# Attention value products of two heads in one call, in the two halves of the array's columns

## The chip, the core and the metric

The kernel runs on one core of one Trainium2 chip. The metric is the device time of one execution in microseconds (us). The engines of the core have their own instruction streams: TensorE (PE) multiplies matrices, VectorE (DVE) and ScalarE (ACT) work on vectors, GpSimd (POOL) is not used for the computation, and SyncE (SP) issues the transfers from the main memory. TensorE writes its results to PSUM, which here is used as eight banks of 128 x 512 fp32 numbers.

## The reference

Two layers, each of a gated feed-forward block, a mixer of three branches, and a second feed-forward block, on 256 positions of width 1024, all in fp32. The mixer's middle branch is latent attention; this is the part that matters here:

```python
def attend(args):                          # for each block of 128 queries
    qn, qp, blk = args
    sc = (einsum('bqhd,bkhd->bhqk', qn, k_nope) + einsum('bqhr,bkr->bhqk', qp, k_pe)) * scale
    sc = where(key_idx[None, :] <= q_idx[:, None], sc, finfo(float32).min)
    p = softmax(sc, axis=-1)
    return einsum('bhqk,bkhd->bqhd', p, v)   # 8 heads, 64 value columns each
o = o.swapaxes(0, 1).reshape(b, s, 8 * 64)
return o @ w_o
```

The other two branches of the mixer are a gated linear recurrence and a depthwise convolution over 31 positions with a layer norm. The three are gated, added and projected.

## The kernel before

All weights are cut into blocks of 128 x 128 and packed in the order of their use, eight blocks to a chunk of 512 KB. A chunk is fetched into one of 7 buffers (`raw`), ACT rounds it to fp32r (`wh`), and DVE computes the rest (`wl`), each into one of 5 buffers. A product of activations and weights is three fp32r matmuls (`gemm`: high by high, high by low, low by high), over 256 columns each. Some small products are done in plain fp32: the sums over rows by a matrix of ones, the attention scores, and the attention values.

The program is recorded first (line 397 is the line of the recorder that issues each instruction, so nearly all rows name it) and then ordered by a planner. TensorE keeps the order in which the program was written. For the other engines `set_due` (line 426) works out backwards, from a table of costs (`cost`, line 366), when each operation is due, and `schedule` (line 468) plays the program through with these costs and takes, on each engine, the ready operation that is due first. A different cost of one kind of matmul moves all due times.

The attention of one layer is spread over eleven steps (`attend`, line 991), which are placed between the tiles of the gates' and output projections by `ATT_AT` (line 38). A step s issues, in this order: the scores of head s; the values of head s - 3; the transposes of head s - 2; the last part of the softmax of head s. The names in the profile: `kt`, `qt` are keys and queries, `s` the softmax's tile (128 queries x 384: the first 128 columns are the first block of queries, which sees only the first 128 keys), `st` its sums, `ptt` its transpose as ACT copies it out of PSUM (two buffers), `vt` the values (keys x heads), `o` the result of two heads in fp32r for the output projection. `xg` and `ya` are activations that the projections around the steps read.

In `values` (line 978) the weights of the array are 64 columns of `vt`, and the output is 64 partitions of a PSUM tile: the even head of a pair goes to partitions 0 to 63, the odd one to 64 to 127. Two matmuls make one head: the first 128 keys by all 256 queries, and the second 128 keys by the second 128 queries. The scores' weights are 128 columns wide, and so are the transposes' and the projections'.

In the mixer's opening, well ahead of the attention, come the convolution branch's input tiles (`c2`, then `c1`, both `c` in the order's rows, `cin` their product), two sums of squares for the norms of queries and keys (`rv`, `ry`, `rt` belong to their reciprocal square roots), and the copies of the rotated keys into `kt`.

Of the kernel before, what the change touches and what calls it, by code (L numbers as in the profile page):

```python
# [12 lines left out]
F32R = mybir.dt.float32r  # L13
# [5 lines left out]
P = 128  # L19
S = 256  # L20
# [5 lines left out]
H = 8  # L26
NOPE, ROPE, VD = 64, 32, 64
# [300 lines left out]
class Op:  # L328


    def __init__(self, at, engine, call, cost, table):
        self.at, self.engine, self.call, self.cost, self.table = at, engine, call, cost, table
        self.before, self.after, self.buffers = set(), set(), []
        self.due, self.start, self.end = 0.0, None, None
# [7 lines left out]
class Program:  # L342
# [23 lines left out]
    def cost(self, engine, method, args, kw, out, ins):  # L366

        n = out.size if isinstance(out, View) else ins[0].size
        sbuf = all(not v.buf.pool.psum for v in ins)
        column = lambda v: isinstance(v, View) and v.size == 1  # L370
        if engine == "sync":
            return max(0.45, n * 4 * P / 360e3)
        if engine == "tensor":
            return n / 2400 + (0.0133 if n < 512 else 0.018) if args[1].buf.dt == F32R else n * 4 / 2400 + 0.005
        if engine == "scalar":
            t = n / 1200 + (0.093 if sbuf else 0.06) + (0.09 if "accum_out" in kw else 0)
            return t + (0.1 if column(kw.get("scale")) else 0) + (0.06 if column(kw.get("bias")) else 0)
        if engine == "gpsimd":
            return 0.15 + n * 0.0018
        if method == "tensor_scalar" and sbuf and n > 16:  # L380
            return n / 1920 + 0.08
        t = (6 if method == "reciprocal" else 1) * n / 960 + 0.069
        return t + (0.06 if sbuf and any(map(column, ins)) else 0)
# [173 lines left out]
def mixer_kernel(ctx: ExitStack, tc: tile.TileContext, ws, xt, par, pos, out):  # L557
    program = Program(tc.nc)
    V, A, G, T, sync = (program.engine(n) for n in ("vector", "scalar", "gpsimd", "tensor", "sync"))
# [11 lines left out]
    def ps():  # L571
        return psp.tile([P, 512], F32, name="ps")
# [3 lines left out]
    def bt(name="bt"):  # L576

        rest = halves.pop(name, None)
        if rest is None:
            both = big.tile([P, 2, S], F32, tag="pair", name=name, parts=2)  # L580
            rest, halves[name] = both[:, 0, :], both[:, 1, :]
        return rest
# [6 lines left out]
    pts = [cst.tile([P, b - a], F32, name=f"par{a}") for a, b in zip(cuts, cuts[1:])]  # L589
# [53 lines left out]
    def split(src, scale=None, name="sp", pool=None):  # L643

        pool = pool or big
        both = pool.tile([P, 2, S], F32R, tag="pair", name=name, parts=2)
        h, lo = both[:, 0, :], both[:, 1, :]
        if scale is None:
            A.activation(h, src, AF.Copy)
            V.tensor_tensor(lo, src, h.bitcast(F32), op=SUB)  # L650
        else:
            A.activation(h, src, AF.Copy, scale=scale)
            V.scalar_tensor_tensor(lo, src, scale, h.bitcast(F32), op0=MUL, op1=SUB)
        return both
# [120 lines left out]
    def mixer(l, norm, nxt):  # L775
# [28 lines left out]
        t = W_IN_ORDER[2]  # L804
# [64 lines left out]
        for i in range(4):  # L869
            A.activation(xin[:, i, :], mm(f"xa{i}"), AF.Identity, bias=bias(f"xa{i}"))  # L870
            t = bt(name="xa")
# [6 lines left out]
        for i in range(4):  # L878
            t = bt(name="gel")
# [12 lines left out]
        for k in range(2):  # L892
            h, lo = W.block("v", l, k, 0, width=4)
            xh, xl = (normed[f"kv{k}"][:, i, :] for i in range(2))
            for t in range(2):
                c = slice(t * P, (t + 1) * P)
# [3 lines left out]
        vt = mixp.tile([P, 2, 512], F32, name="vt", parts=2)  # L900
# [5 lines left out]
        for i in range(4):  # L906
# [6 lines left out]
            c = 4 * l + i  # L913
# [13 lines left out]
        for h in range(H):  # L927
# [3 lines left out]
            t = bt(name="qt")  # L931
# [11 lines left out]
            yas.append(split(gel[i], name="ya"))  # L943


        sm, pts, ot, os_ = {}, {}, {}, {}

        def scores(h):
            k = kt[h % 2][:, h // 2, :]
            acc = ps()  # L950
            T.matmul(acc[:, 0:P], qt[h][:, 0:P], k[:, 0:P], start=True, stop=True)
            T.matmul(acc[:, P:3 * P], qt[h][:, P:S], k, start=True, stop=True)
            s = attp.tile([P, 3 * P], F32, tag="s", name="s")
            st = attp.tile([P, 4], F32, tag="st", name="st")
            mask = whole("mask")
            for i, c in ((0, slice(0, P)), (1, slice(P, 3 * P))):
                V.tensor_tensor_reduce(out=s[:, c], in0=acc[:, c], in1=mask[:, c], scale=1.0, scalar=3e38,
                                       op0=ADD, op1=ALU.min, accum_out=st[:, i:i + 1])
            for i, c in ((0, slice(0, P)), (1, slice(P, 3 * P))):
                A.activation(s[:, c], s[:, c], AF.Exp, bias=st[:, i:i + 1], scale=-1.0, accum_out=st[:, 2 + i:3 + i])  # L960
            sm[h] = (s, st)

        def normalise(h):
            s, st = sm[h]
            V.reciprocal(st[:, 2:4], st[:, 2:4])
            A.activation(s[:, 0:P], s[:, 0:P], AF.Copy, scale=st[:, 2:3])
            A.activation(s[:, P:3 * P], s[:, P:3 * P], AF.Copy, scale=st[:, 3:4])

        def transposes(h):
            s, _ = sm.pop(h)  # L970
            acc = ps()
            for i in range(3):
                T.transpose(acc[:, i * P:(i + 1) * P], s[:, i * P:(i + 1) * P], whole("ident"))
            t = ptp.tile([P, 3 * P], F32, tag="pt", name="ptt")
            A.activation(t, acc[:, 0:3 * P], AF.Copy)
            pts[h] = t

        def values(h):
            p, e = divmod(h, 2)
            if e == 0:  # L980
                ot[p] = ps()[:, :S]
            o = ot[p][64 * e:64 * e + 64]
            t = pts.pop(h)
            T.matmul(o, vt[:, 0, h * VD:(h + 1) * VD], t[:, 0:S], start=True, stop=False)
            T.matmul(o[:, P:S], vt[:, 1, h * VD:(h + 1) * VD], t[:, S:3 * P], start=False, stop=True)
            if e == 1:
                os_[p] = split(ot.pop(p), name="o")

        step = [0]

        def attend():
            s = step[0]
            step[0] += 1
            if s < H:
                scores(s)
            if 0 <= s - 3 < H:
                values(s - 3)
            if 0 <= s - 2 < H:
                transposes(s - 2)
            if s < H:  # L1000
                normalise(s)

        def slot(n):
            if n in ATT_AT:
                attend()
# [65 lines left out]
        while step[0] < H + 3:  # L1071
            attend()
# [18 lines left out]
        pair = [ps() for _ in range(2)]  # L1091
# [85 lines left out]
    for l in range(DEPTH):  # L1177
        mix, second = Norm(f"gm_{l}"), Norm(f"g2_{l}")
        ffn("ffn1_", l, norm, mix, constants if l == 0 else None)
        mixer(l, mix, second)  # L1180
        norm = Norm(f"g1_{l + 1}" if l + 1 < DEPTH else "gf")
        ffn("ffn2_", l, second, norm)
# [33 lines left out]
```

## Time and profile before

| | before |
|---|---|
| device time, median of 3 runs | 1218.55 us (1218.47 to 1218.88) |
| profiled execution | 1218.95 us |
| its span, first to last instruction | 1217.0 us |
| PE busy | 1199.6 us (99%) |
| DVE busy | 952.7 us (78%) |
| ACT busy | 774.5 us (64%) |

The span lies inside the device time; what is around it is start and end of the program. Busy time counts an engine's instructions and not its waits. In the page's timeline by slices PE is at 9 tenths or more in all but the first and last of 40 slices. The ends of matmuls in the trace are modelled, so the length of a matmul's record is longer than the time that the next one has to wait; what a matmul costs is read from the distance of two starts.

### The profile page before, as it was taken

The numbers are of one execution on the slowest core, as the hardware profiler recorded it, in microseconds if no ns is written. First come the engines' busy times: TensorE is split into PE (matmuls) and PEld (weight loads), VectorE is DVE, ScalarE is ACT, GpSimd is POOL, SyncE is SP. The second block draws the span as 40 slices with busy tenths as digits, with TensorE's granted clock in tenths as the row PEclk, the third lists the DMA queues.
The fourth block names the chain that finished last, engine by engine and source line by source line (L and its number), as shares of the span: only waits on it lengthen the run. The fifth ranks groups of instructions, "written<-read, shape, count | busy, mean of one in ns | idle before, by whom it ended". The sixth has DMA issues, their size and how long they took to land.

```text
span 1217.0 us, 21025 instructions
## 1 busy us (share of the span) xinstructions
PE 1199.6 (99%) x8018; PEld 1095.7 (90%) x8018; DVE 952.7 (78%) x1750; ACT 774.5 (64%) x1326; POOL 0.2 (0%) x4
## 2 busy tenths in 40 slices
PE   7999999999999999999999999999999999999997
PEld 6888889999999898888898888899999999988886
DVE  7976667999987986776686676689999699866653
ACT  7655545889657765555465565468896577655552
POOL 0000000000000000000000000000000000000000
PEclk9999999999999999999999999999999999999999
DMA  8655555554445655555555555546544556555540
GB/s 306 222 191 190 181 191 166 191 173 146 157 166 166 197 178 190 189 191 191 178 186 191 191 186 186 186 156 203 174 153 134 179 162 199 184 190 189 190 140 35
DMA packets 61157, 218.17 MB, mean 179 GB/s; under 512 B 6912, under 2 KB 7936, under 8 KB 61056
## 3 DMA queue, kind: packets, MB, share of 16 engines
q1 hardware_dynamic: 61056, 216.82, 54.3%
q8 instruction: 63, 1.03, 0.3%
q14 instruction: 38, 0.31, 0.1%
HBM read 215.75 MB, written 1.05 MB: 178 GB/s over the span
## 4 chain that ended last, share of the span: by engine, by line
PE 98%; DMA 1%; ACT 0%; DVE 0%; SPq 0%; issue 0%; DVEq 0%
PE ps L397 98%; DMA xs<-xt 1%; SPq L397 0%; ACT wh L397 0%; DVE y L397 0%; ACT xg L397 0%; ACT sq L397 0%; DVE wl L397 0%; DVE rt L397 0%; DVEq L1211 0%; ACT ry L397 0%; DVE r L397 0%; DVE rv L397 0%; DVE xs L397 0%
## 5 line engine op out<-in xcount | busy, mean ns | idle before, releaser
L397 PE MATMUL ps<-xg,wh 128*128 128x256 f32 (+1 forms) x3136 | 757.7, 326 | 8.3 <-ACT wh L397 8.3
L397 DVE TENSOR_TENSOR wl<-raw,wh 128x1024 fp32r<-128x1024 f32 (+1 forms) x412 | 498.2, 1212 | 198.1 <-ACT wh L397 196.2
L397 ACT ACTIVATE wh<-raw 128x1024 fp32r<-128x1024 f32 (+1 forms) x412 | 430.9, 1047 | 276.5 <-PE ps L397 153.5
L397 PE MATMUL ps<-xg,wl 128*128 128x256 f32 x2144 | 579.2, 281 | 0.5 <-DVE wl L397 0.5
L397 PEld LDWEIGHTS ps<-xg,wh 128*128 128x128 f32 x3136 | 517.7, 191 | 49.0 <-ACT wh L397 8.5
L397 PEld LDWEIGHTS ps<-xg,wl 128*128 128x128 f32 x2144 | 407.9, 190 | 13.6 <-DVE wl L397 0.9
L397 PE MATMUL ps<-hid,wh 128*128 128x512 f32 (+1 forms) x726 | 247.0, 391 | 0.0
L397 PE MATMUL ps<-hid,wl 128*128 128x256 f32 x704 | 192.7, 281 | 0.0
L397 PEld LDWEIGHTS ps<-hid,wh 128*128 128x128 f32 x726 | 133.2, 188 | 29.1
L397 PEld LDWEIGHTS ps<-hid,wl 128*128 128x128 f32 x704 | 133.1, 189 | 2.7
L397 DVE SCALAR_TENSOR_TENSOR conv<-cin,taps,conv 128x255 f32<-128x255 f32 (+28 forms) x240 | 100.0, 464 | 1.6 <-ACT conv L397 1.3
L397 ACT ACTIVATE s<-s 128x256 f32<-128x256 f32 x88 | 35.8, 414 | 62.6 <-DVE s L397 62.6
L397 ACT ACT_TABLE_LOAD x37 | 47.5, 1283 | 1.3 <-PEq L1205 0.7
L397 ACT ACTIVATE s<-s,st 128x128 f32<-128x128 f32 x64 | 28.0, 451 | 26.7 <-DVE st L397 26.7
L397 PE MATMUL ps<-mg,wh 128*128 128x512 f32 x128 | 44.4, 397 | 0.0
L397 DVE SCALAR_TENSOR_TENSOR xs<-ps,xs 128x256 f32<-128x256 f32 x63 | 26.6, 422 | 22.2 <-PE ps L397 21.4
L397 DVE TENSOR_TENSOR hid<-hid 128x256 fp32r<-128x256 f32 x88 | 36.2, 417 | 0.0
L397 ACT ACTIVATE hid<-hid 128x256 fp32r<-128x256 f32 x88 | 35.3, 409 | 0.0
L397 ACT ACTIVATE sq<-xs 128x256 f32<-128x256 f32 x49 | 19.8, 405 | 23.1 <-DVE xs L397 19.6
L397 PE MATMUL ps<-mg,wl 128*128 128x256 f32 x128 | 33.4, 279 | 0.0
L397 DVE TENSOR_TENSOR u<-ps,u 128x256 f32<-128x256 f32 x72 | 30.1, 418 | 3.7 <-ACT u L397 3.7
L397 DVE TENSOR_TENSOR hid<-u,s 128x256 f32<-128x256 f32 x72 | 30.6, 425 | 2.3
(164 smaller groups left out, 1010.9 us busy)
## 6 DMA issues: line engine op xcount, KB each, us to landing
raw<-ws SPq DMA_DIRECT2D x406, 512.0 KB, 3.4
out<-y SPq DMA_DIRECT2D x4, 256.0 KB, 2.3
par<-par SPq DMA_DIRECT2D x1, 571.0 KB, 8.4
raw<-ws SPq DMA_DIRECT2D x4, 128.0 KB, 3.6
xs<-xt SPq DMA_DIRECT2D x1, 512.0 KB, 7.0
raw<-ws SPq DMA_DIRECT2D x2, 256.0 KB, 7.1
xs<-xt SPq DMA_DIRECT2D x2, 128.0 KB, 2.9
xs<-xt SPq DMA_DIRECT2D x1, 256.0 KB, 4.1
```

The source lines that it names most:

```text
L397: getattr(getattr(self.nc, engine), method)(*map(put, args), **{k: put(v) for k, v in kw.items()})
```

## The change

`values` takes a pair of heads p instead of one head, and is called in the steps 4, 6, 8 and 10 instead of in the steps 3 to 10. In a call the two matmuls over the first keys are issued for the even and then the odd head, and then the two over the second keys. So the even head's values are issued one step later than before, the odd head's in the same step. The planner's cost of a matmul whose weights have 64 columns is multiplied by 0.6. Nothing else is changed in the program's text.

```diff
@@ cost
         if engine == "tensor":
-            return n / 2400 + (0.0133 if n < 512 else 0.018) if args[1].buf.dt == F32R else n * 4 / 2400 + 0.005
+            t = n / 2400 + (0.0133 if n < 512 else 0.018) if args[1].buf.dt == F32R else n * 4 / 2400 + 0.005
+            return t * 0.6 if args[1].shape[-1] == 64 else t
@@ mixer
-        def values(h):
-            p, e = divmod(h, 2)
-            if e == 0:
-                ot[p] = ps()[:, :S]
-            o = ot[p][64 * e:64 * e + 64]
-            t = pts.pop(h)
-            T.matmul(o, vt[:, 0, h * VD:(h + 1) * VD], t[:, 0:S], start=True, stop=False)
-            T.matmul(o[:, P:S], vt[:, 1, h * VD:(h + 1) * VD], t[:, S:3 * P], start=False, stop=True)
-            if e == 1:
-                os_[p] = split(ot.pop(p), name="o")
+        def values(p):
+
+            o = ps()[:, :S]
+            pair = [(64 * e, 2 * p + e, pts.pop(2 * p + e)) for e in range(2)]
+            for c, h, t in pair:
+                T.matmul(o[c:c + 64], vt[:, 0, h * VD:(h + 1) * VD], t[:, 0:S], start=True, stop=False)
+            for c, h, t in pair:
+                T.matmul(o[c:c + 64, P:S], vt[:, 1, h * VD:(h + 1) * VD], t[:, S:3 * P], start=False, stop=True)
+            os_[p] = split(o, name="o")
@@ attend
-            if 0 <= s - 3 < H:
-                values(s - 3)
+            if s >= 4 and s % 2 == 0:
+                values((s - 4) // 2)
```

On PE, step 3 of the first layer's attention, between the tiles of a gate projection, stands so in the order before (the numbers behind names are buffer numbers):

```order
L397 MATMUL ps<-xg,wl 128x256
L397 MATMUL ps<-kt_2643,qt 128x128
L397 MATMUL ps<-kt_2643,qt 128x256
L397 MATMUL ps<-ptt,vt 64x256
L397 MATMUL ps<-ptt,vt 64x128
L397 MATMUL ps<-par_187,s 128x128 x3
L397 MATMUL ps<-xg,wh 128x256 x2
```

and so in the changed kernel, where the values are gone from this step:

```order
L398 MATMUL ps<-xg,wl 128x256
L398 MATMUL ps<-kt_2625,qt 128x128
L398 MATMUL ps<-kt_2625,qt 128x256
L398 MATMUL ps<-par_187,s 128x128 x3
L398 MATMUL ps<-xg,wh 128x256 x2
```

One step later on PE, step 4 of the first layer, the order before has one head's values, like step 3. In the changed kernel the values of two heads stand there:

```order
L398 MATMUL ps<-ya,wl 128x256
L398 MATMUL ps<-kt_2610,qt 128x128
L398 MATMUL ps<-kt_2610,qt 128x256
L398 MATMUL ps<-ptt,vt 64x256 x2
L398 MATMUL ps<-ptt,vt 64x128 x2
L398 MATMUL ps<-par_187,s 128x128 x3
L398 MATMUL ps<-ya,wh 128x256 x2
```

The planner's new cost also moves instructions on DVE and ACT (303 and 110 lines of difference in their orders; PE's has 50). The largest move on ACT is in the opening of the first layer's mixer, where `c` are the evictions of the convolution branch's tiles. Before:

```order
L397 ACTIVATE conv<-cin,par_187,taps_264 128x256
L397 ACTIVATE wh<-raw 128x1024
L397 ACTIVATE c_2581<-ps,hb_261 128x256
L397 ACTIVATE kt_2589<-ps 64x1024
L397 ACT_TABLE_LOAD
L397 ACTIVATE ry<-ps,par_187 128x256 x2
L397 ACTIVATE wh<-raw 128x1024
L397 ACTIVATE kt_2643<-ps 64x1024
L397 ACTIVATE c_2655<-ps,par_187 128x256
```

and in the changed kernel:

```order
L398 ACTIVATE conv<-cin,par_187,taps_264 128x256
L398 ACTIVATE wh<-raw 128x1024
L398 ACT_TABLE_LOAD
L398 ACTIVATE ry<-ps,par_187 128x256 x2
L398 ACTIVATE kt_2610<-ps 64x1024
L398 ACTIVATE kt_2625<-ps 64x1024
L398 ACTIVATE wh<-raw 128x1024
L398 ACT_TABLE_LOAD
L398 ACTIVATE c_2655<-ps,hb_261 128x256
```

The eviction that stood ahead of the copies and the two `ry` now stands behind them and behind a second table load.

## Rows read from the trace of the kernel before

**Rows 1.** The page's head and its first part: busy us, share, instructions.

```profile
span 1217.0 us, 21025 instructions
PE 1199.6 (99%) x8018; PEld 1095.7 (90%) x8018; DVE 952.7 (78%) x1750; ACT 774.5 (64%) x1326; POOL 0.2 (0%) x4
```

**Rows 2.** The page's fourth part, chain that ended last, by engine.

```profile
PE 98%; DMA 1%; ACT 0%; DVE 0%; SPq 0%; issue 0%; DVEq 0%
```

**Rows 3.** Windows: us; busy us (instructions) of PE, PEld, DVE, ACT, POOL; clock; DMA.

```profile
20.00:1200.00 1180.00, 1180.00 (x7889) 1077.87 (x7889) 935.29 (x1708) 758.41 (x1293) 0.00 (x0) 1.00 0.55 179
```

**Rows 4.** Waits of PE after 100 us: us in total, times, longest.

```profile
PE ps L397 <- ACT sq L397: 0.5, 1, 0.5
```

**Rows 5.** The tile vt on PE: ns shortest/median/longest; starts; weights' and operand's forms.

```profile
L397 PE MATMUL ps<-ptt,vt x64: 272/326/431, 303.8 to 962.8; 128*64 128x256 f32 x32, 128*64 128x128 f32 x32
```

**Rows 6.** Timeline of PE, step 2: start us, length us, instruction, how many merged.

```profile
293.40 0.82 PE L397 MATMUL ps<-kt,qt 128*128 128x128 f32 x4
294.06 0.49 PE L397 MATMUL ps<-par,s 128*128 128x128 f32 x3
294.30 0.48 PE L397 MATMUL ps<-xg,wh 128*128 128x256 f32 x2
```

**Rows 7.** Timeline of PE, step 3.

```profile
302.89 0.28 PE L397 MATMUL ps<-xg,wl 128*128 128x256 f32 x1
303.01 0.82 PE L397 MATMUL ps<-kt,qt 128*128 128x128 f32 x4
...
304.86 0.48 PE L397 MATMUL ps<-xg,wh 128*128 128x256 f32 x2
```

**Rows 8.** Timeline of PE, step 8, which has no scores.

```profile
344.21 0.28 PE L397 MATMUL ps<-xg,wl 128*128 128x256 f32 x1
...
345.51 0.48 PE L397 MATMUL ps<-xg,wh 128*128 128x256 f32 x2
```

**Rows 9.** Timeline of PE in step 3's values, in narrow windows.

```profile
303.76 0.43 PE L397 MATMUL ps<-ptt,vt 128*64 128x256 f32 x1
...
304.03 0.38 PE L397 MATMUL ps<-ptt,vt 128*64 128x256 f32 x1
...
304.25 0.38 PE L397 MATMUL ps<-ptt,vt 128*64 128x128 f32 x2
...
304.36 0.27 PE L397 MATMUL ps<-ptt,vt 128*64 128x128 f32 x1
```

**Rows 10.** Timeline of PEld in step 3; in brackets the idle time before.

```profile
303.76 0.62 PEld L397 LDWEIGHTS ps<-ptt,vt 128*64 128x64 f32 x4 [0.33 <-ACT wh L397]
304.56 0.31 PEld L397 LDWEIGHTS ps<-par,s 128*128 128x128 f32 x3 [0.17 <-issue]
```

**Rows 11.** Timeline of ACT: the copy of head 1's transpose.

```profile
306.79 0.48 ACT L397 ACTIVATE ptt<-ps 128x384 f32<-128x384 f32 x1
```

**Rows 12.** Timeline of PE: the first values record of step 4.

```profile
311.45 0.43 PE L397 MATMUL ps<-ptt,vt 128*64 128x256 f32 x1
```

**Rows 13.** Timeline of ACT in the mixer's opening.

```profile
226.15 1.02 ACT L397 ACTIVATE kt<-ps 64x1024 f32<-64x1024 f32 x1
227.19 1.28 ACT L397 ACT_TABLE_LOAD   x1
228.49 0.84 ACT L397 ACTIVATE ry<-ps,par 128x256 f32<-128x256 f32 x2
229.22 1.06 ACT L397 ACTIVATE wh<-raw 128x1024 fp32r<-128x1024 f32 x1
```

**Rows 14.** Windows, two stretches of the first layer's attention.

```profile
280.00:330.00 50.00, 50.00 (x395) 47.16 (x394) 49.80 (x128) 41.81 (x91) 0.00 (x0) 1.00 0.47 150
330.00:367.00 37.00, 37.00 (x293) 34.90 (x292) 30.46 (x60) 20.82 (x36) 0.00 (x0) 1.00 0.50 171
```

**Rows 15.** The tile wl on DVE from 280 to 330 us.

```profile
L397 DVE TENSOR_TENSOR wl<-raw,wh x14: 1203/1220/1227, 280.2 to 327.9; 128x1024 fp32r<-128x1024 f32 x14
```

**Rows 16.** Timeline of PEld: the second load of step 3's values.

```profile
303.82 0.14 PEld L397 LDWEIGHTS ps<-ptt,vt 128*64 128x64 f32 x1
```

More of the change, by code (lines that the diff above doesn't have):

```diff
@@ L943, in recur @@
             yas.append(split(gel[i], name="ya"))
-        sm, pts, ot, os_ = {}, {}, {}, {}
+        sm, pts, os_ = {}, {}, {}
         def scores(h):
```

## Prediction

> **What bounds the kernel now.** I read the page first. Its first part has TensorE (PE) busy for 1199.6 of 1217.0 us, VectorE (DVE) for 78% and ScalarE (ACT) for 64% [rows 1]; its fourth part puts 98% of the chain that ended last on PE [rows 2]. The share of busy time alone could hide short waits, so the next view is the busy time by stretch: from 20 us to 1200 us PE is busy for 1180.00 of 1180.00 us, at a granted clock of 1.00 (the 2.4 GHz level) [rows 3], and the waits of PE after 100 us add up to 0.5 us, one wait, for the last norm's squares [rows 4]. So PE is dense from its start-up to its tail. Time taken out of its instruction stream comes off the end one for one, as long as nothing else becomes late; time put in is added one for one.
>
> **What a values call costs.** The trace has 64 matmul records for the attention values [rows 5]: 16 calls (8 heads, 2 layers) of two fp32 matmuls, each of which is recorded as two passes, each with a weight load of its own. One call is priced by comparing two attention steps. Step 2 has scores and transposes alone: from its first score matmul at 293.40 to the first matmul of the next projection at 294.30 it takes 0.90 us [rows 6]. Step 3 has the values between them: from 303.01 to 304.86, that is 1.85 us [rows 7]. The call costs 0.95 us. The steps without scores agree: from the last matmul ahead of the values to the first one behind the transposes 1.30 us [rows 8], and in step 3 from 302.89 to 304.86, 1.97 us, of which the scores are 0.66 (from 293.40 to 294.06); 1.31 is left. I use 0.95 for all 16: 15.2 us.
>
> What is in the 0.95? The records of one call start at 303.76, 304.03, 304.25 and 304.36 [rows 9]. A pass over 256 columns takes 0.22 (304.03 to 304.25) and one over 128 columns 0.11. So the call's four passes are 2 x 0.22 + 2 x 0.11 = 0.66 us, the same as the four passes of the scores. The other 0.95 - 0.66 = 0.29 us is spent around the passes, and the weight-load rows show where: the values' first load starts 0.33 us after the loads before it had ended, and the transposes' first load 0.17 us after those of the values, while the loads inside a run follow each other [rows 10]. On both sides the form of the weights changes (128 columns, 64 columns, 128 columns), the next load does not run ahead, and the array runs empty: about 0.145 us a change.
>
> The Trainium skill, TensorEngine Tiling (Array Packing), section Tiling Modes, says that a change of tiling mode drains the engine, and that a change of tile within a mode does not. The two gaps agree with its first half; no row here shows the second.
>
> **The change, part by part.**
> 1. Half as many calls. Eight values calls of two heads stand where sixteen of one head stood; the steps 3, 5, 7 and 9 of each layer lose theirs. Eight times the 0.29 around the passes goes: -2.32 us. This part does not need any overlap.
> 2. Two heads in one call. Their passes stand in the order A1 A1 B1 B1 A2 A2 B2 B2 (head A in columns 0 to 63, B in 64 to 127; 1 is the matmul over 256 columns, 2 the one over 128). One after another they are 2 x 0.66 = 1.32 us. No row of before has two halves next to each other in one call, so the overlap is bounded from both sides. The most would be B wholly beside A, 0.66 us a call, 8 x 0.66 = 5.28 us saved. None saves 0. Below that, each change of half could drain as a change of form does: 3 changes a call, 24 in all, 24 x 0.145 = 3.48 us lost. I take the case that follows from the rows' order: passes start in program order, two passes on one half follow each other, a pass on the other half need not wait. Then the first A1 takes 0.22, the second A1 and the first B1 share 0.22, the second B1 shares 0.22 with both A2 (0.11 each), and two B2 follow with 0.11 each: 0.88 us a call, 0.44 saved, 3.52 us over eight calls. If B1's first load is exposed, it adds what the first load of a call adds now, 0.27 - 0.22 = 0.05 us [rows 9]: 0.93 us, 3.12 us saved. I use the middle, 3.32 us.
> 3. The even head's values stand one step later. Each pair now reads the copy of its even head a step later than before, and that of its odd head in the same step as before. The first layer's copy of head 1 ends at 307.27, and the values that read it start at 311.45 [rows 11, 12]: 4.2 us of cover, against some 3 us by which PE gets ahead over a whole layer. The two buffers of these copies suffice, since the pair is read ahead of the same step's transposes. The copies of the results to fp32r for the output projection were made in the same steps (two heads together) before. Cost: nothing.
> 4. The planner. Its cost for the values falls to 0.6, which moves every due time, and so instructions of DVE and ACT in the mixer, also ahead of the attention. The largest move is on ACT early in the mixer: the eviction of the second c2 tile now stands behind an activation-table load, two ry, two kt copies, a weight conversion and a second table load. By the rows of before that is 1.28 + 0.84 + 2 x 1.02 + 1.06 + 1.28 = 6.5 us [rows 13]. Its PSUM bank is held for that much longer, while one projection tile fills a bank in 24 matmuls of 0.12 us (302.89 to 303.01 [rows 7]), 2.9 us: two or three more of the eight banks. I cost it at nothing; if that cover is gone, PE waits for up to the 6.5 us less 2.9 in each layer, 7.2 us, and a gain is the least likely part of it.
> 5. The weight stream. From 280 to 330 us DVE is busy for 49.80 of 50 us [rows 14], and there it converts 14 chunks [rows 15]. A chunk is 8 blocks of 3 matmuls, 2.88 us of PE; the stretch holds the attention steps 0 to 6, at 2 x 0.66 + 0.90 + 4 x 1.85 = 9.6 us, so PE uses (50 - 9.6) / 2.88 = 14.0. Supply and demand are level there, so when PE gets ahead by 2 to 3 us it eats into chunks that are ready, of which up to five have a buffer (14 us of PE work). From 330 to 367 us DVE is busy for 30.46 of 37 us [rows 14] and catches up. Cost: nothing.
>
> Sum: -2.32 - 3.32 = -5.64 us. The profiled execution took 1218.95 us, 1.95 more than its span; 1218.95 - 5.64 = 1213.31. The median of the runs is 0.40 below the profiled one: 1212.9 us.
>
> **The rivals.**
> No overlap. The passes of the two halves run one behind another; only the calls are halved: 1218.55 - 2.32 = 1216.2 us. For it: no row shows two column halves at work together. Against it: weight loads do run beside matmuls here (the load at 303.82 starts while the pass of 303.76 is under way [rows 9, 16]).
> The Trainium skill, TensorE: Matmul & The Clock Gate, section Part 3: Packing small matmuls, speaks for this rival in one place: a weight load overlaps matmuls in flight only when its row group differs, and both halves here use all 128 rows. By that rule B's loads would wait for A. The trace disagrees as it stands, since the load at 303.82 has the same rows as the pass beside it. The same section reports three column tiles 2.38 times as fast, in program order, which speaks for overlap; no run here shows either yet.
>
> Full overlap. B runs wholly beside A, 0.66 us a call: 1218.55 - 2.32 - 5.28 = 1211.0 us. Against it: both passes of A1 stand ahead of B1 in the order, and a stream that starts passes in order can't begin B1 with A1.
>
> A drain at each change of half, slower than before. The place is inside a call, at A1 to B1, B1 to A2 and A2 to B2; the price 0.145 us each, 3.48 us, against 2.32 saved: 1218.55 + 1.16 = 1219.7 us. It decides from 2.32 / 24 = 0.097 us a change on. For it: the array does run empty where the form changes [rows 10]. Against it: the number of columns stays 64 here.
>
> The planner's moves cost. PE waits in the mixer's opening or for a weight chunk, and gives back part or all of the gain: at 1.5 us a layer 1215.9 us, at the 7.2 us of point 4 1220.1 us. For it: 303 lines of DVE's order and 110 of ACT's differ. Against it: the dense rows of PE [rows 3, 4] and cover of several us at each place.
>
> **How the numbers follow.** Overlap by pass 0.61 (its own range 1212.0 to 1214.2), no overlap 0.17, full overlap 0.11, planner's waits 0.07, drains 0.04. A measurement of this kernel can tell 0.2%, 2.4 us, from no change. Overlap of either kind is faster by more; no overlap, at 2.3 us, lies just inside, and I give a quarter of it and half of the planner's case to faster: 0.79. Slower by over 0.2% needs waits of over 8 us or drains at twice their price: 0.04. The rest, 0.17, is within. The range goes from 1210.9 (full overlap) to 1216.5 (no overlap).
>
> **What would show it.** In the profile after: eight runs of eight values records, in steps 4, 6, 8 and 10; steps 3, 5 and 7 at 0.90 us from scores to the next projection, as step 2 now. Right, if within a run the first record of B1 starts about 0.22 us after the first of A1 together with A1's second, and the run takes 0.88 to 0.93 us. Wrong by no overlap, if eight starts stand 0.22 or 0.11 apart in a row, 1.32 us; by drains, if there is a further gap at each change of half; by the planner, if PE shows waits after 20 us.

## The result, and the profile after

The changed kernel takes 1210.88 us (median of 4 runs, 1210.50 to 1212.03), against 1218.69 us before (1218.47 to 1218.88): a ratio of 0.9938, with an interval from 0.9926 to 0.9951. It is faster by 7.8 us. Forecast were 1212.9 us and a range from 1210.9 to 1216.5, so the direction was right and the gain 2 us larger than the forecast: the time lies at the lower end of the range, which had been drawn at full overlap. The rival named full overlap, at 1211.0 us, is the one that happened.

The page of the changed kernel has the same engines at the same shares (compare [rows 1]):

```profile
span 1208.7 us, 21026 instructions
PE 1191.8 (99%) x8018; PEld 1092.3 (90%) x8018; DVE 951.2 (79%) x1750; ACT 773.7 (64%) x1326; POOL 0.2 (0%) x4
```

PE is as dense as it was [rows 3]: 1170.00 busy us of 1170. DVE is now busy for all 50 us of the stretch in which it had 49.80 [rows 14], and PE does not wait there. The rows are the windows of the changed kernel, and the one wait of PE after 100 us (compare [rows 4]):

```profile
20.00:1190.00 1170.00, 1170.00 (x7872) 1072.41 (x7871) 932.41 (x1702) 756.73 (x1292) 0.00 (x0) 1.00 0.54 180
280.00:330.00 50.00, 50.00 (x410) 48.30 (x410) 50.00 (x129) 42.27 (x91) 0.00 (x0) 1.00 0.48 152
330.00:367.00 37.00, 37.00 (x309) 35.95 (x308) 31.44 (x60) 20.64 (x37) 0.00 (x0) 1.00 0.56 186
```

```profile
PE ps L398 <- ACT sq L398: 0.5, 1, 0.5
```

Step 3 of the attention, which has lost its values, on PE (compare [rows 7]): 302.25 to 303.16 is 0.91 us, where step 3 took 1.85.

```profile
302.25 0.82 PE L398 MATMUL ps<-kt,qt 128*128 128x128 f32 x4
302.91 0.49 PE L398 MATMUL ps<-par,s 128*128 128x128 f32 x3
303.16 0.36 PE L398 MATMUL ps<-xg,wh 128*128 128x256 f32 x1
```

Step 4, which now has the values of two heads:

```profile
308.99 0.82 PE L398 MATMUL ps<-kt,qt 128*128 128x128 f32 x4
309.74 0.87 PE L398 MATMUL ps<-ptt,vt 128*64 128x256 f32 x8
310.54 0.55 PE L398 MATMUL ps<-par,s 128*128 128x128 f32 x3
310.84 0.36 PE L398 MATMUL ps<-ya,wh 128*128 128x256 f32 x1
```

308.99 to 310.84 is 1.85 us, with eight values records where step 3 of before had four in the same 1.85. The second head costs nothing that two decimals show. Four narrow windows on the timeline of this call show how; each row merges the values records that touch its window:

```profile
309.74 0.43 PE L398 MATMUL ps<-ptt,vt 128*64 128x256 f32 x1
...
309.74 0.44 PE L398 MATMUL ps<-ptt,vt 128*64 128x256 f32 x2
...
309.74 0.65 PE L398 MATMUL ps<-ptt,vt 128*64 128x256 f32 x3
...
309.74 0.65 PE L398 MATMUL ps<-ptt,vt 128*64 128x256 f32 x4
```

The windows begin at 309.735, 309.76, 310.001 and 310.015. The row of the second window holds the first two passes, both over 256 columns and begun within 0.02 us; two passes of one head start 0.27 us apart [rows 9], so one of them is the other head's. One pass has begun by 309.744, two by 309.76, three by 310.009, four by 310.1: the passes come in twos. The second of a two ends 0.01 us after the first (0.44 for 0.43), and the next two follow where the second pass of a lone head stood before, about 0.27 us after the first [rows 9]. The weight loads of the call show the same gaps as before at both its ends, 0.33 and 0.17 us [rows 10], now around eight loads:

```profile
309.74 0.63 PEld L398 LDWEIGHTS ps<-ptt,vt 128*64 128x64 f32 x8 [0.33 <-ACT gate L398]
310.54 0.31 PEld L398 LDWEIGHTS ps<-par,s 128*128 128x128 f32 x3 [0.17 <-issue]
```

So eight steps lost 1.85 - 0.91 = 0.94 us each, 7.5 us in all. The two profiled executions are 1218.95 - 1210.61 = 8.34 us apart. Most of the other 0.8 us is in the start-up, where one input transfer on the chain of waits landed sooner; first the row of before, then that of after:

```profile
4.48 6.97 DMA xs<-xt
```

```profile
4.48 6.21 DMA xs<-xt
```

That is 0.76 us of a transfer that the change does not touch. It differs from run to run (6.53 and 6.57 us in two of the kernels below), and the medians, 7.6 to 7.8 us apart, hold little of it.

### The profile page after: what moved, and what is told of

Same layout as the page of the kernel before. It is cut to its first block, busy times and chain, and to the rows that moved or that the text cites. A ratio compares the mean times of both kernels' runs of the same rounds, so it can differ in the third digit from the quotient of the medians.

```text
span 1208.7 us, 21026 instructions
## 1 busy us (share of the span) xinstructions
PE 1191.8 (99%) x8018; PEld 1092.3 (90%) x8018; DVE 951.2 (79%) x1750; ACT 773.7 (64%) x1326; POOL 0.2 (0%) x4
## 4 chain that ended last, share of the span: by engine, by line
PE 98%; DMA 1%; ACT 0%; DVE 0%; SPq 0%; issue 0%; DVEq 0%
PE ps L398 98%; DMA xs<-xt 1%; SPq L398 0%; ACT wh L398 0%; DVE y L398 0%; ACT xg L398 0%; ACT sq L398 0%; DVE wl L398 0%; DVE rt L398 0%; DVEq L1211 0%; ACT ry L398 0%; DVE r L398 0%; DVE rv L398 0%; DVE xs L398 0%
## 5 line engine op out<-in xcount | busy, mean ns | idle before, releaser
L398 DVE SCALAR_TENSOR_TENSOR conv<-cin,taps,conv 128x251 f32<-128x251 f32 (+28 forms) x240 | 99.8, 466 | 1.6 <-ACT conv L398 1.3
```

What stands on the lines that cost most here:

```text
L398: getattr(getattr(self.nc, engine), method)(*map(put, args), **{k: put(v) for k, v in kw.items()})
```

## The experiments

Two things were to be told apart: how much the halved number of calls gives by itself, and how the overlap of the halves comes about.

**Both heads in the same half.** The pairs and their order stay; only the half changes.

```diff
-            o = ps()[:, :S]
-            pair = [(64 * e, 2 * p + e, pts.pop(2 * p + e)) for e in range(2)]
+            pair = [(ps()[0:64, 0:S], 2 * p + e, pts.pop(2 * p + e)) for e in range(2)]
...
+            both = tt("ob")
+            for e in range(2):
+                A.activation(both[64 * e:64 * e + 64], pair[e][0], AF.Copy)
```

> The pairs stay together and in the order A1 B1 A2 B2, but both heads' products use columns 0 to 63, into two PSUM tiles, and ACT copies them together into one tile. Theory H (the gain has two terms, half as many changes of form, and two halves at work together): the calls take 1.32 us of passes instead of 0.66, 8 x 0.66 = 5.3 us more than the changed kernel, about 1216.2 us, 2.3 us under the kernel before. Rival (the pairing alone makes the gain, whatever the half): 0.66 us a call, about 1210.9 us.

Measured: 1216.12 us against 1218.43 before (ratio 0.9980, 0.9971 to 0.9989), 2.31 us less than before and 5.2 us more than the changed kernel. Step 4 on PE:

```profile
309.30 0.82 PE L398 MATMUL ps<-kt,qt 128*128 128x128 f32 x4
310.05 1.51 PE L398 MATMUL ps<-ptt,vt 128*64 128x256 f32 x8
311.49 0.55 PE L398 MATMUL ps<-par,s 128*128 128x128 f32 x3
311.80 0.48 PE L398 MATMUL ps<-ya,wh 128*128 128x256 f32 x2
```

The step takes 2.50 us instead of 1.85: the eight passes run one behind another. This is the case without overlap, forecast at 1216.2 us, and it shows the two terms apart: 2.3 us from the calls, 5.2 us from the halves. By the interval of this ratio the calls' 2.3 us lie anywhere from 1.3 to 3.5 us; the step says the same with less noise, since a call of eight passes one behind another costs 2.50 - 0.91 = 1.59 us, where two calls of before cost 2 x 0.95 = 1.90, and eight times the 0.31 between them is 2.5 us.

**Program order A1 A2 B1 B2.** One line less: the first loop issues both matmuls of a head.

```diff
             for c, h, t in pair:
                 T.matmul(o[c:c + 64], vt[:, 0, h * VD:(h + 1) * VD], t[:, 0:S], start=True, stop=False)
-            for c, h, t in pair:
                 T.matmul(o[c:c + 64, P:S], vt[:, 1, h * VD:(h + 1) * VD], t[:, S:3 * P], start=False, stop=True)
```

> The pairs stay together in steps 4, 6, 8 and 10, but the order inside a call is A1 A2 B1 B2 (head A in columns 0 to 63, head B in 64 to 127; 1 is the matmul over 256 columns, 2 the one over 128). Theory L (the array's queue looks ahead: a pass waits only for passes on its own half, wherever it stands in the call): A2 does not hold B1 back, a call's passes take 0.66 us as in the changed kernel, about 1210.9 us. Theory N (passes start in program order, and only neighbours overlap): A1 takes 0.44, then A2 (0.22) runs beside B1 (0.44), then B2 0.22: 1.10 us a call, 8 x 0.44 = 3.5 us more than the changed kernel, about 1214.4 us. Rival without any overlap in this order: 1.32 us a call, 1216.2 us.

Measured: 1210.86 us (ratio 0.9937, 0.9923 to 0.9952), the changed kernel's time. Step 4 on PE, and then the shapes of the passes that touch 309.78 to 309.90 (instruction, count, busy us, mean ns):

```profile
309.00 0.82 PE L398 MATMUL ps<-kt,qt 128*128 128x128 f32 x4
309.75 0.88 PE L398 MATMUL ps<-ptt,vt 128*64 128x256 f32 x8
310.56 0.55 PE L398 MATMUL ps<-par,s 128*128 128x128 f32 x3
310.87 0.48 PE L398 MATMUL ps<-ya,wh 128*128 128x256 f32 x2
```

```profile
L398 PE MATMUL ps<-ptt,vt 128*64 128x256 f32 x2 | 0.4, 430 | 0.0
```

The step takes 1.87 us. At 309.78 two passes over 256 columns are under way, both long as a call's first pass is (430 ns). They can't be the two passes of A1, which share a half and follow each other by 0.22 us; one is B1's, and it started ahead of three passes that stand before it in the program. Theory L held here, and theory N, whose starts in program order are what the prediction used, fell.

The Trainium skill, TensorE: Matmul & The Clock Gate, section Part 3: Packing small matmuls, says that matmuls start and end in strict program order, and that a weight load overlaps matmuls in flight only when its row group differs. For two column halves these runs differ from both: here B1 overtook, and in the changed kernel the loads of both halves run beside each other's passes with the same 128 rows. The measurement decides. The row of the loads in the changed kernel, from a window that begins at 309.75, holds the first loads of both halves, while the row of matmuls above has the first pass begun at 309.74:

```profile
309.74 0.14 PEld L398 LDWEIGHTS ps<-ptt,vt 128*64 128x64 f32 x2 [0.33 <-ACT gate L398]
```

**How far does the look-ahead reach?** Four heads in one call, in the steps 6 and 10, came first; two buffers fewer for temporaries make room for four copies.

```diff
-    xgp, big, tmp = pool("xgp", 16), pool("big", 22), pool("tmp", 8)
-    mixp, attp, ptp = pool("mixp", 1), pool("attp", 3), pool("ptp", 2)
+    xgp, big, tmp = pool("xgp", 16), pool("big", 22), pool("tmp", 6)
+    mixp, attp, ptp = pool("mixp", 1), pool("attp", 3), pool("ptp", 4)
...
+            o = {p: ps()[:, :S] for p in ps_}
+            heads = [(p, 64 * e, 2 * p + e, pts.pop(2 * p + e)) for p in ps_ for e in range(2)]
+            for p, c, h, t in heads:
+                T.matmul(o[p][c:c + 64], vt[:, 0, h * VD:(h + 1) * VD], t[:, 0:S], start=True, stop=False)
+            for p, c, h, t in heads:
+                T.matmul(o[p][c:c + 64, P:S], vt[:, 1, h * VD:(h + 1) * VD], t[:, S:3 * P], start=False, stop=True)
...
-            if s >= 4 and s % 2 == 0:
-                values((s - 4) // 2)
+            if s in (6, 10):
+                values((0, 1) if s == 6 else (2, 3))
```

> Values of four heads in one call, in the steps 6 and 10, with four buffers for the transposes' copies (two buffers fewer in the pool of temporaries pay for them). Theory (each call costs 0.29 us around its passes, and halves overlap wholly): 4 calls instead of 8, 4 x 0.29 = 1.16 us less than the changed kernel, about 1209.7 us; passes of a call 1.32 us for four heads. Rival (fewer temporaries or the later values make PE wait): PE shows waits after 20 us, 1210.9 us or more.

Measured: 1209.49 us (ratio 0.9926, 0.9906 to 0.9946). Step 6 on PE:

```profile
319.55 0.82 PE L398 MATMUL ps<-kt,qt 128*128 128x128 f32 x4
320.30 1.52 PE L398 MATMUL ps<-ptt,vt 128*64 128x256 f32 x16
321.75 0.55 PE L398 MATMUL ps<-par,s 128*128 128x128 f32 x3
322.05 0.48 PE L398 MATMUL ps<-xg,wh 128*128 128x256 f32 x2
```

From 319.55 to 322.05, 2.50 us: the call costs 2.50 - 0.91 = 1.59, two calls of two heads 2 x 0.94 = 1.88. The 0.29 of a call's two changes of form went, as expected. In step 10, where projections stand on both sides, the call can be compared by its length alone; first two heads in the changed kernel, then four heads here, each with the row behind it:

```profile
360.10 0.87 PE L398 MATMUL ps<-ptt,vt 128*64 128x256 f32 x8
360.90 0.50 PE L398 MATMUL ps<-xg,wh 128*128 128x256 f32 x2
```

```profile
358.80 1.52 PE L398 MATMUL ps<-ptt,vt 128*64 128x256 f32 x16
360.25 0.51 PE L398 MATMUL ps<-xg,wh 128*128 128x256 f32 x2
```

0.80 and 1.45 us: two more heads add 0.65 us, their passes, and nothing around them.

Then the same four heads, with all passes of one half ahead of all passes of the other:

```diff
-            heads = [(p, 64 * e, 2 * p + e, pts.pop(2 * p + e)) for p in ps_ for e in range(2)]
+            heads = [(p, 64 * e, 2 * p + e, pts.pop(2 * p + e)) for e in range(2) for p in ps_]
             for p, c, h, t in heads:
                 T.matmul(o[p][c:c + 64], vt[:, 0, h * VD:(h + 1) * VD], t[:, 0:S], start=True, stop=False)
-            for p, c, h, t in heads:
                 T.matmul(o[p][c:c + 64, P:S], vt[:, 1, h * VD:(h + 1) * VD], t[:, S:3 * P], start=False, stop=True)
```

> Four heads in one call as in the run of four heads, but all passes of the two heads in columns 0 to 63 (eight passes, 1.32 us) stand ahead of all passes of the two heads in columns 64 to 127. The run with the order A1 A2 B1 B2 showed that four passes of the other half do not hold a pass back, only by 13 ns. Theory L (each half has its own stream, which is filled in program order some 3 ns a pass ahead): the second half starts 8 x 3.3 = 26 ns behind the first, a call's passes take 1.32 + 0.03 us, the time is within 0.3 us of the run of four heads. Rival Q (the look-ahead reaches only a few passes): the second half starts later, up to 1.32 us, 4 calls x 1.32 = 5.3 us more, up to 1214.8 us.

Measured: 1212.54 us in its one run, 3 us more than with the heads in turn; 0.4 of this is the first transfer (6.57 us here, 6.18 there). Theory L, that a half's stream has no limit to its reach, fell: the trace shows the place. The call and its successor on PE, and then narrow windows that begin at 321.36, 321.39 and 321.40:

```profile
320.69 2.22 PE L398 MATMUL ps<-ptt,vt 128*64 128x256 f32 x16
322.84 0.55 PE L398 MATMUL ps<-par,s 128*128 128x128 f32 x3
```

```profile
321.17 0.38 PE L398 MATMUL ps<-ptt,vt 128*64 128x128 f32 x2
...
321.17 0.60 PE L398 MATMUL ps<-ptt,vt 128*64 128x128 f32 x3
...
321.17 0.65 PE L398 MATMUL ps<-ptt,vt 128*64 128x128 f32 x4
```

From the call's start to the transposes it is 2.15 us, where the call with the heads in turn took 1.45 (320.30 to 321.75): 0.70 more, and four such calls make 2.8 us. Two passes begin within 0.01 us at 321.39 to 321.40, 0.70 us after the call's start. Passes of one half stand 0.11 us or more apart, so they are one of each half: the fifth pass of the first half (behind two passes over 256 and two over 128 columns, 0.66 us and the first load), and with it the first pass of the other half, the ninth in the program. It did not go with the fourth pass, when four passes of the first half were waiting; it went with the fifth, when three were. All four calls of this kernel lose the same 0.70 us. In the order A1 A2 B1 B2 three passes were waiting as well.

All eight heads in one call in step 10, in turn and then half by half, check this at another length (`ptp` 8 and `raws` 5, `tmp` 8 as before, and `if s == 10: values(range(4))`; the second with the edit just above):

> All eight heads in one call in step 10 (heads in turn in the two halves), eight buffers for the transposes' copies, five raw weight buffers instead of seven. Theory (0.29 us for each call's two changes of form): 2 calls instead of 4, 0.58 us less than the run of four heads, about 1208.9 us. Rival (the output projection waits for four pairs that come at once, or fewer raw buffers make PE wait for weights): waits of PE after 20 us, 1209.5 us or more.

> All eight heads in one call in step 10, with eight buffers for the transposes' copies (two raw weight buffers fewer pay for them), and all sixteen passes of the heads in columns 0 to 63 (2.6 us) ahead of the sixteen of the other half. Theory L: the second half starts 16 x 3.3 = 53 ns behind the first; about 1209 us. Rival Q: the reach of the look-ahead ends between 8 and 16 passes, and the second half starts up to 2.6 us late, 2 calls x 2.6 = 5.2 us more.

Measured in turn: 1209.25 us (ratio 0.9925, 0.9909 to 0.9941). Half by half: 1212.83 us in its one run. The calls on PE, each with the row behind it, first in turn:

```profile
357.17 2.82 PE L398 MATMUL ps<-ptt,vt 128*64 128x256 f32 x32
359.92 0.51 PE L398 MATMUL ps<-xg,wh 128*128 128x256 f32 x2
```

```profile
357.20 4.82 PE L398 MATMUL ps<-ptt,vt 128*64 128x256 f32 x32
361.95 0.51 PE L398 MATMUL ps<-xg,wh 128*128 128x256 f32 x2
```

2.75 and 4.75 us, and 2.75 is 1.30 more than the 1.45 of four heads: again passes alone. The 2.0 us between them are the time of twelve passes of the first half (three times 0.66): by this length the other half began with the thirteenth, when again three were waiting. Theory L's 0.05 us is far off, the rival's upper bound of 2.6 near.

**The planner's old cost.** The changed kernel without the factor of 0.6.

```diff
-            return t * 0.6 if args[1].shape[-1] == 64 else t
+            return t
```

> The changed kernel with the planner's old cost for the values. Theory (the planner's moves on DVE and ACT cost and gain nothing, as PE waits for neither): PE as in the changed kernel, 22 attention stretches of the same lengths, about 1210.9 us. Rival (the new cost is part of the gain, or hides a wait): PE shows waits after 20 us and the time is 0.5 to 3 us above the changed kernel.

Measured: 1210.87 us (ratio 0.9937, 0.9922 to 0.9952). The planner's moves on DVE and ACT neither cost nor gain.

**Four heads once more**, the same kernel measured again:

> The run of four heads in a call once more, with more rounds, since it is the fastest kernel so far: 1209.5 us again, 1.2 to 1.4 us less than the changed kernel.

Measured: 1209.77 us (ratio 0.9929, 0.9916 to 0.9942), 0.3 us more than the first time. The call of all eight heads, with 1209.25 us, is the fastest kernel here, about 1.6 us faster than the changed one; its lead over four heads, 0.5 us when measured side by side, is what two calls less should give (2 x 0.29), but the intervals overlap.

## Why the prediction was right or wrong

What bounds the kernel: right. PE stayed dense, and the time taken from its stream (7.5 us in the eight steps) came off the end (7.6 to 7.8 us).

Half as many calls, -2.32 us: right. With both heads in one half the kernel was 2.31 us faster than before, and with fewer calls still each call saved took about the same: 0.29 us by the steps with four heads, 0.26 by the time with eight (0.52 us for two calls).

Two heads in one call, -3.32 us: this is the term that was mis-sized. It measured 5.25 us (1216.12 against 1210.87 of the kernel with the old cost, measured side by side), next to the upper bound of 5.28. The step that failed is the assumption that passes start in program order, so that B1 has to wait for the second pass of A1. The order A1 A2 B1 B2 at the same time shows that it does not hold, and the calls sorted by half show up to where: a pass of the other half goes ahead of three waiting ones. In the changed kernel it is enough that it goes ahead of one. The bound of the nearest row, that B runs wholly beside A, was in the range, but was given 0.11, on the argument about order that fell. By the prediction's own sign it was wrong here: B1 was to start about 0.22 us after A1, and starts about 0.01 after it; the call's passes were to take 0.88 to 0.93 us, and a step with them takes the 1.85 us that it took with a lone head's 0.66. That the total still lies at the end of the range is luck in part: the range of the mechanism that was forecast, 1212.0 to 1214.2 us, missed it, and only the wider one, drawn out to a rival, holds it.

The even head's values one step later, and the weight stream: right as far as PE shows, which waits for neither. DVE, at 50.00 of 50 us, had no time to spare in that stretch.

The planner's moves, at nothing: right, by the kernel with the old cost.

The rivals: no overlap fell, and so did drains at a change of half, since the passes come in twos without a gap. The drains at a change of form are as forecast.

## What to carry to other kernels

Where a small product uses half of the array's columns, try its partner in the other half next to it: here two such fp32 products cost what one cost (0.94 us a call against 0.95), and each call less saved the two changes of form around it. This pays as it did here only where TensorE is what the kernel waits for. Keep the partners near each other in the program; sorted by half they lost the overlap (3 us) beyond the reach of three waiting passes. Before forecasting an overlap from the order of a stream, ask whether the order of starts in the trace was ever tested by two instructions that could have passed each other: in the trace of before there were none.

## What the runs showed of the hardware that was not expected

A matmul on one half of the columns started ahead of three waiting passes on the other half (order A1 A2 B1 B2), and not ahead of four (calls sorted by half). Whether the limit counts passes, what is left of two fp32 matmuls of two passes each, or loads and passes together, these runs can't tell; nor do they show what in the engine sets it. When it went, it followed the other half's pass by about 0.01 us. A change between weights of 128 and of 64 columns costs about 0.29 us for the way there and back with four, eight or sixteen passes between (0.95 - 0.66, 0.94 - 0.66 and 1.59 - 1.32), and thirty-two passes add only their own time (2.75 - 1.45 = 1.30 us in step 10).
